# One hybrid pooling and SSD layer on one core: branch tiles loaded and split during two gate blocks, a third gate buffer, an earlier state update

## The chip, the core and the metric

The kernel runs on one core of a Trainium2 chip. The metric is the device time of one execution in microseconds (us). The kernel before was run three times: 2823.08, 2823.70 and 2825.81 us, median 2823.7. A separate execution was profiled, and its trace is what all views below come from.

The core has five engines with an instruction stream each, which wait for one another by semaphores. PE (TensorE) multiplies matrices into PSUM, DVE (VectorE) and ACT (ScalarE) work on elements, POOL (GpSimd) and SP (SyncE) mostly issue DMA transfers. [...]

## The reference

One layer of a streaming encoder is computed for 384 rows (256 of a prompt and 8 streams of 16), 2048 channels, in float32:

```
u  = RMSNorm(x);  P = u @ w_in        # pool | z | xBC | dt | gates
A  = scale * pool_w(pooling(P.pool))                      # branch A
Y  = chunked SSD scan(conv(P.xBC), dt) + d_skip * x
B  = group RMSNorm(Y * silu(z))                           # branch B
m  = sigmoid(g_A) * (A @ w_pool_proj) + sigmoid(g_B) * (B @ w_ssd_proj)
x += RMSNorm(m @ w_out)
x += RMSNorm(relu(RMSNorm(x) @ w_up)^2 @ w_down)
```

The scan's states of the running streams are updated and returned as well. The change touches the gate `sigmoid(g_B)`, the last state update of the scan, and the way branch B gets to its product with `w_ssd_proj`.

## The kernel before

Every float32 product is made of three: both operands are split into a high part (rounded to float32r by an ACT copy) and a low part (the rest, by a DVE subtraction), and PE multiplies high by high, high by low and low by high (lines 107 to 109 in `moving`, 76 to 78 in `mm3`).

**Weights.** They stream from DRAM in tiles of 128 x 1024, 512 KB each. `wfetch` (line 59) loads one over the queue of SP into one of three `w` buffers, `wsplit` (line 64) makes `wh` on ACT (line 68) and `wl` on DVE (line 69), with three buffers each. `moving` (line 99) goes through such tiles with one accumulator of 128 x 512 for each of three blocks of 128 rows (`three`, line 133): 18 matmuls a tile. After the last tile it calls `done(b)` for each block. A `hook` is a pair: after the matmuls of the tile of that number a function is called.

**Order.** The program is written with a scheduler that orders the instructions of each engine by their place in the text and by when it expects their inputs, so loads, copies and subtractions of later tiles move ahead as far as buffers allow. Matmuls of the scan stage are tied in written order (`behind`, `chain`). Memory comes from pools: a tile on the bytes of an earlier one waits for that one's users. PSUM has two banks `mm` (`mmtile`) and six banks `ss` (`sstile`), handed out in turn. `main` (line 172) holds on the right side of SBUF the input split in two (`xg`), and small tiles, among them the gate output `gbt`, two buffers.

**The stages around the change.** The scan runs over eight groups of two pairs (loop at line 776). After the last group, in the turn `g == G` (line 777):

- `dside` scales the last pair's state `hs` by its decay on DVE (line 701).
- `gate_b(0)` (line 519) multiplies `xg` with the first 512 columns of the gate weights, eight tiles. Its `done` writes the sigmoid of each of three blocks into `gbt` (ACT, line 524), and POOL stores that to DRAM, `gb_scr` (line 525).
- `state` (line 708) updates `hs`: eight small matmuls `su` into four `ss` banks (line 716), four additions on DVE (line 725), and a store on POOL (line 729). It reads `xst`, loaded by eight DMAs of SP (line 675).
- `t_yT`, `t_Y`, `t_pp` and `final` end the last pair; `gate_b(1)` follows, then `finish` (line 757), which normalises the last group and stores its four tiles of branch B in `a_scr` on POOL (line 765). The other 28 tiles are there already.
- `gate_b(2)` and `gate_b(3)`, and `main` is closed (line 859).

Then the product of branch B: 32 tiles `ar` are loaded from `a_scr` over SP (line 884) into three buffers, split into `abh` (ACT, line 887) and `abl` (DVE, line 888), which stay. Four blocks `pj_sp` with 16 weight tiles each follow (line 901), each with `ma` and `gb` read back from DRAM (lines 893 and 894), and from the second on `merge` as hook, which transposes what the block before gave.

Of the kernel before, what the change touches and what calls it, by code (L numbers as in the profile page):

```python
# [6 lines left out]
F32 = mybir.dt.float32  # L7
F32R = mybir.dt.float32r
# [6 lines left out]
P = 128  # L15
# [18 lines left out]
def build(ctx, tc, io):  # L34
# [18 lines left out]
    def sstile(name):  # L53
        return pss.tile([P, 512], F32, tag="ss", name=name)
# [44 lines left out]
    def moving(o, units, lhs, tail, done, pool=None, own=0, hook=None):  # L99
        nk = 2 * len(units)  # L100
        n = len(units)

        def mm(b, wh, wl, k, k2):
            t = slice(b * P, b * P + P)
            c = slice(k2 * 512, k2 * 512 + 512)
            mh, ml = lhs[k][0][:, t], lhs[k][1][:, t]
            te.matmul(o[b], mh, wh[:, c], start=k == 0, stop=False)  # L107
            te.matmul(o[b], mh, wl[:, c], start=False, stop=False)  # L108
            last[0] = te.matmul(o[b], ml, wh[:, c], start=False, stop=k == nk - 1)  # L109

        for kp in range(n - tail):
            wh, wl = wload(*units[kp])
            with behind(last[0] if chain[0] else None):
                for k2 in range(2):
                    for b in range(3):
                        mm(b, wh, wl, kp * 2 + k2, k2)
            if hook and kp == hook[0]:
                hook[1]()
        w = [wload(*units[kp]) for kp in range(n - tail, n - own)]
        for kp in range(n - own, n):  # L120
            f, name = wfetch(*units[kp])
            h = pool.tile([P, 1024], F32R, name=f"eh_{name}")
            l = pool.tile([P, 1024], F32R, name=f"el_{name}")
            s.activation(h, f, AF.Copy)
            v.tensor_tensor(l, f, h.bitcast(F32), ALU.subtract)
            w.append((h, l))
        for b in range(3):
            for i, (wh, wl) in enumerate(w):
                for k2 in range(2):
                    mm(b, wh, wl, (n - tail + i) * 2 + k2, k2)  # L130
            done(b)

    def three(name):
        return [sstile(f"{name}_{b}") for b in range(3)]
# [167 lines left out]
    with tc.tile_pool(name="phc", bufs=1, reuse_waits="tile") as pc, tc.tile_pool(name="phc2", bufs=2, reuse_waits="tile") as pc2:  # L302
# [174 lines left out]
        for nb in range(4):  # L477
# [3 lines left out]
            if nb == 0:  # L481
                dt_turn(srcs)

    with tc.tile_pool(name="phd", bufs=2, reuse_waits="tile") as pd, tc.tile_pool(
        name="phd1", bufs=1, reuse_waits="tile"
    ) as pd1:
# [13 lines left out]
        def conv(ui, c, tag, nb):  # L500
# [14 lines left out]
            o = pd.tile([P, T], F32, tag=tag, name=f"xs{c}", bufs=nb)  # L515
            s.activation(o, a, AF.Silu, bias=vec[:, V_CB + c : V_CB + c + 1])
            return o

        def gate_b(nb):
            o = three(f"pj_gb{nb}")  # L520

            def done(b):
                t = small.tile([P, 512], F32, tag="gbt", name=f"gbt{nb}_{b}", bufs=2)
                s.activation(t, o[b], AF.Sigmoid, scale=yx[:, b : b + 1])
                gp.dma_start(gb_scr[nb][:, b], t)

            moving(o, [(io["w_gb"][nb, kp], f"gb{nb}_{kp}") for kp in range(8)], xg, 0, done)

        def lump(fn):
            with behind(last[0]):  # L530
# [174 lines left out]
                ALU.mult,  # L705
            )

        def state(S):
            def t_su():
                hs = S.hs.rearrange("p (r h) n -> p h r n", h=2)  # L710
                for r2 in (0, 2):
                    su = [sstile(f"su{S.nm}_{r2}_{h}") for h in range(2)]
                    for r in range(2):
                        for h in range(2):
                            t = slice(h * 64, h * 64 + 64)
                            i = te.matmul(
                                su[h][:, r * 256 : r * 256 + 256],
                                S.D.bs[t, r2 + r, :],
                                S.xst[t, r2 + r, :],
                                start=True,  # L720
                                stop=True,
                            )
                    for h in range(2):
                        hr = hs[:, h, r2 : r2 + 2]
                        v.tensor_tensor(hr, hr, su[h].rearrange("p (r n) -> p r n", r=2), ALU.add)
                return i

            lump(t_su)
            gp.dma_start(io["new_ssm_s"][S.qd], S.hs)
# [46 lines left out]
        for g in range(G + 1):  # L776
            if g == G:
                dside(prev.p[1])
                gate_b(0)
                state(prev.p[1])  # L780
                py = sstile("pp_last")
                lump(lambda: t_yT(prev.p[1]))
                lump(lambda: t_Y(prev.p[1]))
                lump(lambda: t_pp(prev.p[1], py))
                final(prev.p[1])
                gate_b(1)
                finish(prev)
                break
            u0 = 17 + g * 10
            D = Pair()  # L790
            D.g = g
            D.p = [pair(D, jp) for jp in range(2)]
            D.xs, D.zs = [], []
            D.BT = conv(u0, 32 + g, "BT", 2)
            pload(D.p[0])
            if g:
                dside(prev.p[1])
            D.CT = conv(u0 + 1, 40 + g, "CT", 2)
            if g:
                state(prev.p[1])  # L800
            D.xs.append(conv(u0 + 2, g * 4, "xs", 6))
            cload(D.p[0])
            cside(D)
            D.xs.append(conv(u0 + 3, g * 4 + 1, "xs", 6))
            D.xs.append(conv(u0 + 4, g * 4 + 2, "xs", 6))
            S = D.p[0]
            lump(lambda: t_cb(D))
            mside(D)
            lump(lambda: t_trB(D))
            bside(D)  # L810
            lump(lambda: t_trx(S))
            if g:
                lump(lambda: t_yT(prev.p[1]))
                lump(lambda: t_Y(prev.p[1]))
            S.py = sstile(f"py{S.nm}")
            lump(lambda: t_yi(S))
            if g:
                lump(lambda: t_pp(prev.p[1], S.py))
            if g:
                final(prev.p[1])  # L820
            xside(S)
            D.xs.append(conv(u0 + 5, g * 4 + 3, "xs", 6))
            eside(S, 0)

            def zproj(j):
                ps = proj(in_units(u0 + 6 + j), xg, f"z{g}_{j}")
                z = pd.tile([P, T], F32, tag="zs", name=f"zs{g}_{j}", bufs=7)
                v.tensor_tensor(z, ps, rstd, ALU.mult)
                s.activation(z, z, AF.Silu)
                D.zs.append(z)  # L830

            zproj(0)
            if g:
                finish(prev)
            pload(D.p[1])
            eside(S, 1)
            zproj(1)
            dside(S)
            zproj(2)
            state(S)  # L840
            cload(D.p[1])
            zproj(3)
            S1 = D.p[1]
            lump(lambda: t_trx(S1))
            lump(lambda: t_yT(S))
            lump(lambda: t_Y(S))
            S1.py = sstile(f"py{S1.nm}")
            lump(lambda: t_yi(S1))
            lump(lambda: t_pp(S, S1.py))
            final(S)  # L850
            xside(S1)
            eside(S1, 0)
            eside(S1, 1)
            prev = D
        gate_b(2)
        gate_b(3)
        chain[0] = False
        gp.dma_start(io["new_conv"], cst_)
    main.close()

    mpool = ExitStack()
    mp = mpool.enter_context(tc.tile_pool(name="mp", bufs=1, side="right", reuse_waits="tile"))
    ms_, mtok = [], [None]

    def merge():
# [11 lines left out]
        if len(ms_) == KD:  # L877
            mp.tile([P, 120], F32, name="pad_m")

    with tc.tile_pool(name="phe", bufs=1, reuse_waits="tile") as pe1, tc.tile_pool(name="phe2", bufs=3, reuse_waits="tile") as pe2:  # L880
        ab = []
        for i in range(32):
            a = pe2.tile([P, T], F32, tag="ar", name=f"ar{i}")
            sy.dma_start(a, a_scr[i])
            h = pe1.tile([P, T], F32R, name=f"abh{i}")
            l = pe1.tile([P, T], F32R, name=f"abl{i}")
            s.activation(h, a, AF.Copy)
            v.tensor_tensor(l, a, h.bitcast(F32), ALU.subtract)
            ab.append((h, l))
        for nb in range(4):  # L890
            ma = mp.tile([P, 3, 512], F32, tag="mar", name=f"mar{nb}", bufs=1)
            gb = pe2.tile([P, 3, 512], F32, tag="gbr", name=f"gbr{nb}", bufs=1)
            sy.dma_start(ma, ma_scr[nb])
            sy.dma_start(gb, gb_scr[nb])
            o = three(f"pj_sp{nb}")
# [2 lines left out]
                v.tensor_tensor(gb[:, b], o[b], gb[:, b], ALU.mult)  # L898
                v.tensor_tensor(ma[:, b], ma[:, b], gb[:, b], ALU.add)

            moving(o, [(io["w_ssd"][nb, kp], f"sp{nb}_{kp}") for kp in range(16)], ab, 0, done, hook=(3, merge) if nb else None)
            mtok[0] = ma

    res = ctx.enter_context(tc.tile_pool(name="res", bufs=1, reuse_waits="tile"))
# [25 lines left out]
    with tc.tile_pool(name="phf", bufs=1, side="right", reuse_waits="tile") as pf, tc.tile_pool(  # L930
# [19 lines left out]
        for nb in range(4):  # L950
# [5 lines left out]
            def done(b):  # L956
# [20 lines left out]
                done,  # L977
                pk,
                5 if nb == 3 else 0,
                None if nb else (3, merge),  # L980
            )
            lastwo = last[0]
        phk.close()
# [316 lines left out]
```

## Time and profile before

| what | value |
|---|---|
| median of three runs | 2823.7 us |
| profiled execution | 2822.85 us |
| its span, first to last instruction | 2821.0 us |
| mean granted TensorE clock | 0.998 |
| PE busy | 2800.5 us |
| DVE busy | 1543.5 us |
| ACT busy | 1087.3 us |
| moved by DMA | 451.39 MB, 160 GB/s |

The gate blocks `pj_gb` run from 1204.72 to 1340.57 us of the span, with a short stretch of the scan after the first, and the first block of `pj_sp` starts at 1347.26 us.

A row of the timeline is the start, the duration (of a run of instructions, if x is over 1), the engine, the line, the operation, written tile, read tiles, shapes and count; in brackets the idle time of the engine ahead of it and whose end ended it. A row of the groups has busy time, mean duration in ns, and the idle time before. PEld is PE loading its stationary operand; SPq is the queue of SP. A matmul's duration overlaps the next one's, so the distance of two starts tells the pace.

### The profile page before, as it was taken

Reading aid. Unit: us, or ns where it says so; the run is one execution under the profiler, and the core shown is the slowest. Engines: PE = TensorE matmul, PEld = TensorE weight load, DVE = VectorE, ACT = ScalarE, POOL = GpSimd, SP = SyncE. Lnnn points to the kernel's source line nnn. Section 1 sums busy time; section 2 is a strip of 40 time slices with the busy share of each in tenths; the row PEclk is TensorE's granted clock in tenths of the full one; section 3 lists DMA queues with packets and bytes.
Section 4 is the critical chain, followed back from the end, with each engine's and each line's share of the span. In section 5 each row is a group of like instructions: output and inputs, shape, how many; then the busy total and the mean of one; then the engine's idle time right before and its main releaser. Section 6 shows DMA issues by size and latency. Waiting matters only on the chain.

```text
span 2821.0 us, 39010 instructions
## 1 busy us (share of the span) xinstructions
PE 2800.5 (99%) x15663; PEld 2546.3 (90%) x15663; DVE 1543.5 (55%) x2219; ACT 1087.3 (39%) x1586; POOL 87.5 (3%) x143
## 2 busy tenths in 40 slices
PE   9999999999999999999999999999999999999998
PEld 8998889999999999988788888989899998989897
DVE  6574336788787878844434335534444444444445
ACT  5443224454444545433422234433233333323233
POOL 0000000010000001000000000000000000000000
PEclk9999999999999999999999999999999999999999
DMA  7444445655656566544744543433434433333433
GB/s 272 131 127 143 145 139 198 204 196 183 215 202 212 192 210 200 201 160 161 236 149 149 181 154 113 142 127 127 128 127 131 129 128 127 128 127 127 128 127 126
DMA packets 140933, 451.39 MB, mean 160 GB/s; under 512 B 17808, under 2 KB 39632, under 8 KB 135760
## 3 DMA queue, kind: packets, MB, share of 16 engines
q1 hardware_dynamic: 132624, 412.97, 44.7%
q0 software_dynamic: 8128, 35.93, 3.5%
q8 instruction: 123, 2.02, 0.3%
q14 instruction: 58, 0.48, 0.1%
HBM read 407.11 MB, written 41.72 MB: 159 GB/s over the span
## 4 chain that ended last, share of the span: by engine, by line
PE 95%; issue 3%; DVE 0%; DMA 0%; POOL 0%; ACT 0%; SPq 0%; DVEq 0%; POOLq 0%; ACTq 0%
PE pj_up L77 6%; PE pj_up L78 6%; PE pj_up L76 6%; PE wd L109 6%; PE wd L108 6%; PE wd L107 6%; PE pj_x L76 5%; PE pj_x L78 5%; PE pj_x L77 5%; PE pj_z L76 3%; PE pj_z L78 3%; PE pj_z L77 3%; PE pj_sp L107 3%; PE pj_sp L108 3%; PE pj_sp L109 3%
## 5 line engine op out<-in xcount | busy, mean ns | idle before, releaser
L76 PE MATMUL pj_up<-x1h,wh_up 128*128 128x384 f32 x1024 | 342.6, 335 | 0.5 <-ACT x1h L1026 0.5
L78 PE MATMUL pj_up<-x1h,wl_up 128*128 128x384 f32 x1024 | 342.3, 334 | 0.7 <-DVE wl_up L69 0.7
L77 PE MATMUL pj_up<-x1l,wh_up 128*128 128x384 f32 x1024 | 342.3, 334 | 0.6 <-DVE x1l L1031 0.6
L69 DVE TENSOR_TENSOR wl_wd<-w_wd,wh_wd 128x1024 fp32r<-128x1024 f32 x127 | 155.7, 1226 | 261.9 <-ACT wh_wd L68 261.9
L108 PE MATMUL wd<-wl_wd,hh 128*128 128x512 f32 x762 | 296.6, 389 | 0.0
L109 PE MATMUL wd<-wh_wd,hl 128*128 128x512 f32 x762 | 296.6, 389 | 0.0
L107 PE MATMUL wd<-wh_wd,hh 128*128 128x512 f32 x762 | 296.3, 389 | 0.0
L68 ACT ACTIVATE wh_wd<-w_wd 128x1024 fp32r<-128x1024 f32 x127 | 134.9, 1062 | 350.6 <-PE wd L109 284.0
L69 DVE TENSOR_TENSOR wl_up<-w_up,wh_up 128x1024 fp32r<-128x1024 f32 x128 | 156.9, 1226 | 198.5 <-ACT wh_up L68 198.4
L68 ACT ACTIVATE wh_up<-w_up 128x1024 fp32r<-128x1024 f32 x128 | 136.0, 1063 | 323.7 <-PE pj_up L77 259.7
L76 PE MATMUL pj_x<-xgh,wh_x 128*128 128x384 f32 x768 | 258.9, 337 | 0.0
L78 PE MATMUL pj_x<-xgh,wl_x 128*128 128x384 f32 x768 | 256.6, 334 | 0.0
L77 PE MATMUL pj_x<-xgl,wh_x 128*128 128x384 f32 x768 | 256.6, 334 | 0.0
L77 PEld LDWEIGHTS pj_up<-x1l,wh_up 128*128 128x128 f32 x1024 | 192.2, 188 | 1.4 <-DVE x1l L1031 1.2
L76 PEld LDWEIGHTS pj_up<-x1h,wh_up 128*128 128x128 f32 x1024 | 192.2, 188 | 1.3 <-ACT x1h L1026 1.0
L78 PEld LDWEIGHTS pj_up<-x1h,wl_up 128*128 128x128 f32 x1024 | 192.2, 188 | 1.0 <-DVE wl_up L69 1.0
L76 PE MATMUL pj_z<-xgh,wh_z 128*128 128x384 f32 x512 | 171.9, 336 | 0.0
L78 PE MATMUL pj_z<-xgh,wl_z 128*128 128x384 f32 x512 | 171.1, 334 | 0.0
L77 PE MATMUL pj_z<-xgl,wh_z 128*128 128x384 f32 x512 | 171.0, 334 | 0.0
L108 PEld LDWEIGHTS wd<-wl_wd,hh 128*128 128x128 f32 x762 | 143.0, 188 | 29.8 <-DVE wl_wd L69 0.2
L109 PEld LDWEIGHTS wd<-wh_wd,hl 128*128 128x128 f32 x762 | 143.0, 188 | 29.7
L107 PEld LDWEIGHTS wd<-wh_wd,hh 128*128 128x128 f32 x762 | 143.0, 188 | 29.5
(318 smaller groups left out, 5729.7 us busy)
## 6 DMA issues: line engine op xcount, KB each, us to landing
w_up<-w_up SPq DMA_DIRECT2D x128, 512.0 KB, 3.4
w_wd<-w_down SPq DMA_DIRECT2D x128, 512.0 KB, 3.4
w_x<-w_in SPq DMA_DIRECT2D x96, 512.0 KB, 4.7
w_z<-w_in SPq DMA_DIRECT2D x64, 512.0 KB, 4.0
w_sp<-w_ssd SPq DMA_DIRECT2D x64, 512.0 KB, 3.4
w_ga<-w_ga SPq DMA_DIRECT2D x32, 512.0 KB, 3.5
w_pp<-w_pp SPq DMA_DIRECT2D x32, 512.0 KB, 3.4
hs<-ssm SPq DMA_DIRECT2D x16, 1024.0 KB, 6.0
```

Source lines behind the costliest of these rows:

```text
L68: s.activation(h, w, AF.Copy)
L69: v.tensor_tensor(l, w, h.bitcast(F32), ALU.subtract)
L76: te.matmul(out, wh, xh, start=first, stop=False)
L77: te.matmul(out, wh, xl, start=False, stop=False)
L78: return te.matmul(out, wl, xh, start=False, stop=last)
L107: te.matmul(o[b], mh, wh[:, c], start=k == 0, stop=False)
L108: te.matmul(o[b], mh, wl[:, c], start=False, stop=False)
L109: last[0] = te.matmul(o[b], ml, wh[:, c], start=False, stop=k == nk - 1)
```

## The change

1. `gate_b` moves ahead of the scan stage. Its output gets a pool of its own, `gbp`, with three buffers in place of two.
2. `moving` takes as hook a dictionary from tile numbers to functions.
3. The last state update is called as a hook of the first gate block, after its fifth tile (number 4). Its first two `su` tiles, and the tile `pp_last`, come from the two `mm` banks.
4. `gate_b(2)` and `gate_b(3)` move behind the end of the scan stage's pools, into the stage of branch B. After each of their 16 weight tiles a hook `aload` loads and splits two branch tiles.
5. `main` is closed, and the pool `mp` opened, after these blocks; the read-back tile `gbr` gets a pool `phe3` that opens after that.

```diff
@@ moving
-            if hook and kp == hook[0]:
-                hook[1]()
+            if hook and kp in hook:
+                hook[kp]()
@@ ahead of the scan stage
+    gbp = main.enter_context(tc.tile_pool(name="gbp", bufs=3, side="right"))
+
+    def gate_b(nb, hook=None):
+        o = three(f"pj_gb{nb}")
+
+        def done(b):
+            t = gbp.tile([P, 512], F32, tag="gbt", name=f"gbt{nb}_{b}")
+            s.activation(t, o[b], AF.Sigmoid, scale=yx[:, b : b + 1])
+            gp.dma_start(gb_scr[nb][:, b], t)
+
+        moving(o, [(io["w_gb"][nb, kp], f"gb{nb}_{kp}") for kp in range(8)], xg, 0, done, hook=hook)
@@ scan stage (the old gate_b, with bufs=2 in the pool small, goes)
-        def state(S):
+        def state(S, tiles=(sstile, sstile)):
             def t_su():
                 hs = S.hs.rearrange("p (r h) n -> p h r n", h=2)
-                for r2 in (0, 2):
-                    su = [sstile(f"su{S.nm}_{r2}_{h}") for h in range(2)]
+                for r2, tile_ in zip((0, 2), tiles):
+                    su = [tile_(f"su{S.nm}_{r2}_{h}") for h in range(2)]
...
                 dside(prev.p[1])
-                gate_b(0)
-                state(prev.p[1])
-                py = sstile("pp_last")
+                gate_b(0, {4: lambda: state(prev.p[1], (mmtile, sstile))})
+                py = mmtile("pp_last")
...
-        gate_b(2)
-        gate_b(3)
-        chain[0] = False
         gp.dma_start(io["new_conv"], cst_)
-    main.close()
-
-    mpool = ExitStack()
-    mp = mpool.enter_context(tc.tile_pool(name="mp", bufs=1, side="right", reuse_waits="tile"))
@@ stage of branch B
-        for i in range(32):
-            a = pe2.tile([P, T], F32, tag="ar", name=f"ar{i}")
-            sy.dma_start(a, a_scr[i])
-            h = pe1.tile([P, T], F32R, name=f"abh{i}")
-            l = pe1.tile([P, T], F32R, name=f"abl{i}")
-            s.activation(h, a, AF.Copy)
-            v.tensor_tensor(l, a, h.bitcast(F32), ALU.subtract)
-            ab.append((h, l))
+
+        def aload():
+            for i in (len(ab), len(ab) + 1):
+                a = pe2.tile([P, T], F32, tag="ar", name=f"ar{i}")
+                sy.dma_start(a, a_scr[i])
+                h = pe1.tile([P, T], F32R, name=f"abh{i}")
+                l = pe1.tile([P, T], F32R, name=f"abl{i}")
+                s.activation(h, a, AF.Copy)
+                v.tensor_tensor(l, a, h.bitcast(F32), ALU.subtract)
+                ab.append((h, l))
+
+        for nb in (2, 3):
+            gate_b(nb, {kp: aload for kp in range(8)})
+        chain[0] = False
+        main.close()
+        mp = mpool.enter_context(tc.tile_pool(name="mp", bufs=1, side="right", reuse_waits="tile"))
+        pe3 = phe.enter_context(tc.tile_pool(name="phe3", bufs=1, reuse_waits="tile"))
         for nb in range(4):
             ma = mp.tile([P, 3, 512], F32, tag="mar", name=f"mar{nb}", bufs=1)
-            gb = pe2.tile([P, 3, 512], F32, tag="gbr", name=f"gbr{nb}", bufs=1)
+            gb = pe3.tile([P, 3, 512], F32, tag="gbr", name=f"gbr{nb}")
```

More of the change, by code (lines that the diff above doesn't have):

```diff
@@ L517, in conv @@
             return o
[L519 to L527, printed above, removed]
         def lump(fn):
@@ L878, in merge @@
             mp.tile([P, 120], F32, name="pad_m")
-    with tc.tile_pool(name="phe", bufs=1, reuse_waits="tile") as pe1, tc.tile_pool(name="phe2", bufs=3, reuse_waits="tile") as pe2:
+    mpool = ExitStack()
+    with ExitStack() as phe:
+        pe1 = phe.enter_context(tc.tile_pool(name="phe", bufs=1, reuse_waits="tile"))
+        pe2 = phe.enter_context(tc.tile_pool(name="phe2", bufs=3, reuse_waits="tile"))
         ab = []
-        for i in range(32):
-            a = pe2.tile([P, T], F32, tag="ar", name=f"ar{i}")
-            sy.dma_start(a, a_scr[i])
-            h = pe1.tile([P, T], F32R, name=f"abh{i}")
-            l = pe1.tile([P, T], F32R, name=f"abl{i}")
-            s.activation(h, a, AF.Copy)
-            v.tensor_tensor(l, a, h.bitcast(F32), ALU.subtract)
-            ab.append((h, l))
+        def aload():
[13 more added lines that the diff above has]
+        pe3 = phe.enter_context(tc.tile_pool(name="phe3", bufs=1, reuse_waits="tile"))
         for nb in range(4):
             ma = mp.tile([P, 3, 512], F32, tag="mar", name=f"mar{nb}", bufs=1)
-            gb = pe2.tile([P, 3, 512], F32, tag="gbr", name=f"gbr{nb}", bufs=1)
+            gb = pe3.tile([P, 3, 512], F32, tag="gbr", name=f"gbr{nb}")
             sy.dma_start(ma, ma_scr[nb])
@@ L899, in done @@
                 v.tensor_tensor(ma[:, b], ma[:, b], gb[:, b], ALU.add)
-            moving(o, [(io["w_ssd"][nb, kp], f"sp{nb}_{kp}") for kp in range(16)], ab, 0, done, hook=(3, merge) if nb else None)
+            moving(o, [(io["w_ssd"][nb, kp], f"sp{nb}_{kp}") for kp in range(16)], ab, 0, done, hook={3: merge} if nb else None)
             mtok[0] = ma
@@ L979, in build @@
                 5 if nb == 3 else 0,
-                None if nb else (3, merge),
+                None if nb else {3: merge},
             )
```

## The prediction

> **What bounds the kernel now.** I read the page first, then the list of waits, then the timeline at the two places of the change.
>
> ```profile
> PE 2800.5 (99%) x15663; PEld 2546.3 (90%) x15663; DVE 1543.5 (55%) x2219; ACT 1087.3 (39%) x1586; POOL 87.5 (3%) x143
> ...
> PE 95%; issue 3%; DVE 0%; DMA 0%; POOL 0%; ACT 0%; SPq 0%; DVEq 0%; POOLq 0%; ACTq 0%
> ```
>
> PE is busy for 2800.5 of 2821.0 us and makes up 95% of the chain that ended last. The change removes no matmul, so all it can win is PE idle time (20.5 us in the whole span) and matmuls that run slowly after an idle stretch. The list of waits says where one large piece lies (total us, times, longest):
>
> ```profile
> ACT abh L887 <- DMA ar<-a_scr: 22.2, 13, 2.9
> ...
> PE pj_sp L107 <- ACT abh L887: 6.7, 1, 6.7
> ```
>
> The second row is the largest PE wait that the list names: 6.7 us, once, before the first branch product. The timeline around it:
>
> ```profile
> 1339.24 1.37 ACT L524 ACTIVATE gbt<-pj_gb,yx 128x512 f32<-128x512 f32 x2 [1.66 <-PE pj_gb L109]
> ...
> 1339.30 1.33 SPq L884 DMA_DIRECT2D ar<-a_scr  x3
> ...
> 1340.18 0.39 PE L109 MATMUL pj_gb<-wh_gb,xgl 128*128 128x512 f32 x1
> 1340.23 1.22 POOL L525 DMA_DIRECT2D gb_scr<-gbt  x2 [27.01 <-ACT gbt L524]
> ...
> 1346.11 0.69 ACT L524 ACTIVATE gbt<-pj_gb,yx 128x512 f32<-128x512 f32 x1 [4.45 <-DMA gb_scr<-gbt]
> 1346.69 1.34 ACT L887 ACTIVATE abh<-ar 128x384 fp32r<-128x384 f32 x3
> ...
> 1347.26 0.79 PE L107 MATMUL pj_sp<-wh_sp,abh 128*128 128x512 f32 x1 [6.69 <-ACT abh L887]
> ...
> 1351.17 0.40 PE L107 MATMUL pj_sp<-wh_sp,abh 128*128 128x512 f32 x1
> ```
>
> The last gate block ends on PE at 1340.57 (1340.18 + 0.39). Its third sigmoid needs one of two gbt buffers, and those are still being written to DRAM; ACT stands in order behind that until 1346.11, and the first branch copy (abh) stands behind the sigmoid. The branch loads were themselves only issued at 1339.30. PE starts at 1347.26, and nine steps bring it to 1351.17, 0.43 us each.
>
> **The change part by part.** *The wait before the branch product.* With branch tiles split ahead and a buffer for each sigmoid, the tenth pj_sp matmul (1351.17) would start ten ordinary steps after the last pj_gb start. One weight tile is 18 matmuls and takes 4.09 us (weight copies at 1332.44 and 1336.53, quoted below, each let go by PE), so a step is 0.227: 1340.18 + 2.27 = 1342.45. That is 8.72 us gained: 6.85 of idle (1347.26 against 1340.41) and 1.87 of slow steps. The bounds are nothing, if another wait ends as late, and 8.72.
>
> The windows show the slow steps as a lower granted clock (columns: PE, PEld, DVE, ACT, POOL busy and count; clock; DMA share; GB/s):
>
> ```profile
> 1276.00:1309.00 33.00, 33.00 (x147) 27.32 (x146) 16.84 (x22) 10.54 (x12) 3.78 (x7) 1.00 0.53 177
> 1309.00:1340.30 31.30, 31.30 (x140) 25.81 (x138) 9.81 (x8) 9.09 (x11) 0.61 (x2) 1.00 0.44 144
> 1340.30:1347.30 7.00, 0.31 (x3) 0.04 (x1) 1.28 (x2) 2.56 (x5) 1.22 (x3) 0.78 0.91 336
> 1347.30:1364.00 16.70, 16.70 (x66) 13.70 (x67) 8.30 (x13) 7.67 (x13) 0.33 (x1) 0.89 0.79 266
> 1364.00:1420.00 56.00, 56.00 (x249) 46.39 (x248) 31.50 (x43) 24.66 (x35) 0.00 (x0) 1.00 0.65 199
> ```
>
> The clock is 1.00 in the gate blocks and 0.78 and 0.89 around the wait. [...]
>
> *The last state update, moved after the fifth of eight weight tiles of gate block 0.* Where it stands now, and the same eight matmuls inside a stream of projections:
>
> ```profile
> 1190.56 0.33 PE L77 MATMUL pj_z<-xgl,wh_z 128*128 128x384 f32 x1
> 1190.73 0.34 PE L78 MATMUL pj_z<-xgh,wl_z 128*128 128x384 f32 x1
> 1191.00 0.75 PE L716 MATMUL su<-xst,bst 64*128 64x256 f32 x8
> ...
> 1191.95 0.34 PE L77 MATMUL pj_z<-xgl,wh_z 128*128 128x384 f32 x1
> ```
>
> ```profile
> 1236.33 1.37 ACT L524 ACTIVATE gbt<-pj_gb,yx 128x512 f32<-128x512 f32 x2 [0.36 <-PE pj_gb L109]
> ...
> 1237.27 0.39 PE L109 MATMUL pj_gb<-wh_gb,xgl 128*128 128x512 f32 x1
> ...
> 1237.58 0.74 PE L716 MATMUL su<-xst,bst 64*128 64x256 f32 x8
> ...
> 1238.12 2.48 DVE L725 TENSOR_TENSOR hs<-hs,su 128x512 f32<-128x512 f32 x4 [2.19 <-PE su L716]
> ...
> 1238.87 0.44 PE L587 MATMUL Y<-cst,yis 128*128 128x128 f32 x2 [0.54 <-DVE hs L725]
> ```
>
> From the last gate matmul to Y is 1.60 us now; 0.54 of it PE waits for DVE, since Y takes a PSUM bank that the state update holds. Inside a stream the update costs 1191.95 - 1190.73 = 1.22 less two ordinary steps of 0.17 (1190.56 to 1190.73) = 0.88. Gate to Y then takes one step plus the 0.08 of the change of kind (1237.58 - 1237.27 - 0.23), 0.31. So 1.60 - 0.88 - 0.31 = 0.41 us gained; the ends are nothing (the update waits inside the block) and 0.54. In the new place Y's second bank is that of the block's first sigmoid, done at 1237.02 (1236.33 + half of 1.37), before Y can start. The update's inputs:
>
> ```profile
> 1209.60 4.14 SPq L675 DMA_DIRECT2D xst<-x_scr  x8
> ...
> 1210.59 2.29 DVE L701 TENSOR_TENSOR hs<-hs,decb 128x2048 f32<-128x2048 f32 x1
> ```
>
> Issued by 1213.74 and scaled by 1212.88; the new place is three tiles before 1237.3, about 1225, so 11 us are left for the landing. The four DVE additions (2.48 us) and the state store on POOL move 12 us forward with it; DVE, busy 55% of the span, has room for them.
>
> *Branch tiles in gate blocks 2 and 3.* Work is moved, none added: 32 loads on SP, 32 copies on ACT, 32 subtractions on DVE, two of each per weight tile, against what the weights cost already:
>
> ```profile
> L69 DVE TENSOR_TENSOR wl_gb<-w_gb,wh_gb 128x1024 fp32r<-128x1024 f32 x32 | 39.1, 1224 | 66.4 <-ACT wh_gb L68 66.4
> ...
> L888 DVE TENSOR_TENSOR abl<-ar,abh 128x384 fp32r<-128x384 f32 x32 | 16.7, 556 | 19.4 <-ACT abh L887 19.4
> ...
> L887 ACT ACTIVATE abh<-ar 128x384 fp32r<-128x384 f32 x32 | 15.9, 523 | 22.2 <-DMA ar<-a_scr 22.2
> ```
>
> Per 4.09 us: ACT 1.06 (the weight copy) + 2 x 0.52 = 2.1, DVE 1.22 + 2 x 0.56 = 2.34. In block 2, with the normalisation, DVE has 16.84 + 16 x 0.56 = 25.7 of 33 us. Sixteen loads of 197 KB in 33 us add 95 GB/s to 177 and 144; the chip gave 266 in the first stretch of pj_sp and 336 in the wait. So throughput suffices, and the question is order. A branch copy that waits for its load holds the next weight copy behind it on ACT, with it the weight subtraction on DVE, the release of the weight buffer to SP, and PE at the end. The margin can be read, and so can what the same mix made of it in pj_sp:
>
> ```profile
> 1332.44 1.06 ACT L68 ACTIVATE wh_sp<-w_sp 128x1024 fp32r<-128x1024 f32 x1 [3.02 <-PE pj_gb L109]
> 1336.53 1.06 ACT L68 ACTIVATE wh_sp<-w_sp 128x1024 fp32r<-128x1024 f32 x1 [3.02 <-PE pj_gb L109]
> ...
> 1369.74 1.06 ACT L68 ACTIVATE wh_sp<-w_sp 128x1024 fp32r<-128x1024 f32 x1 [0.17 <-PE pj_sp L109]
> ...
> 1397.70 1.04 ACT L68 ACTIVATE wh_sp<-w_sp 128x1024 fp32r<-128x1024 f32 x1
> ```
>
> The split that starts at 1332.44 ends at about 1334.8 and is used at 1340.41: 5.6 us of margin. From 1369.74 to 1397.70 six further splits ran with three branch tiles each, 4.66 us apiece against PE's 4.09: the split fell 3.4 us behind, and PE was busy 56.00 of 56.00 us. So the cost in gate blocks is nothing if two tiles go with each split (three buffers in 4.66 us allow 2.6 per 4.09). If all 32 run three to a split it is 10.7 x 0.57 = 6.1, 0.5 beyond the margin; with three sigmoids in between (half of 1.37 each, 2.1) and, as an estimate, two DVE instructions of 0.56 from the normalisation in the way (1.1), it is 3.7. I take nothing, by the row of 56.00, and keep 3.7 for the range.
>
> **Sum.** 8.72 + 0.41 = 9.1 us. The profiled execution took 2822.85 us (span 2821.0), 0.85 below the median of 2823.7; from the median, 2814.6. Faster here means by over 0.2%, 5.6 us, below 2818.1; within that bound a measurement of this kernel can't tell it from no change.
>
> **The rivals.** *Slower: a loop closes through SP and ACT.* If the program's order puts the two branch loads behind the weight load that waits for a buffer, and the branch copies ahead of the weight copy that frees it, each weight tile runs: three issues (about 0.4 each, from 1.33 for three), landing, two copies (1.05), weight copy (1.06), subtraction (1.22). Issue and landing:
>
> ```profile
> L884 SPq DMA_DIRECT2D ar<-a_scr x32: 319/320/423, 1339.3 to 1393.9; - x32
> ...
> DMA to landing us min/median/max: 2.7/3.6/5.4
> ```
>
> With 3.6 for the landing (2.7 to 5.4) that is 8.1 us against 4.09. Over all 16 tiles PE loses 16 x 4.0 - 5.6 = 58 us and the kernel takes 2823.7 + 58 - 9 = 2873; it turns slower once about four tiles run so ((9.1 + 5.6) / 4.0), beyond the bound from five. Against it: in pj_sp the branch loads stood one step ahead, and ACT waited 2.9 us for one at the longest. For it: loads now alternate strictly with weights, and ACT is in order. [...]
>
> *The wait shrinks but stays.* Branch tiles lie on bytes of the tiles before them. Where another stage changes, its first loads come late (SP rows and PE rows of one timeline):
>
> ```profile
> 1613.17 1.37 SPq L929 DMA_DIRECT2D x<-x_tok  x3
> ...
> 1614.10 0.39 PE L109 MATMUL pj_sp<-wh_sp,abl 128*128 128x512 f32 x1
> ```
>
> The next stage's x1 comes only as the last pj_sp matmul is near, though DMA had room. If the branch loads still begin at 1339.30, only the sigmoid's wait goes: the first tile lands by 1342.9 to 1344.7 and PE starts after one copy, 1343.4 to 1345.2, 2.1 to 3.9 us earlier than now. With 0.4 that is 2.5 to 4.3, so 2819.4 to 2821.2, unless the shorter gap also saves the 1.87. A softer form, loads only from the middle of block 2, near 1293, needs 32 x 1.55 (4.66 / 3) = 50 us, to 1343: no loss, as product k needs only tiles 2k and 2k + 1.
>
> *A new wait eats part.* The gate rows read back for pj_sp (gbr) now lie, by the order in which the pools open and close, on bytes of the gate output buffers, so their load may hold SP until the last gate store has landed, with the fourth weight tile of pj_sp behind it.
>
> ```profile
> w_sp<-w_ssd SPq DMA_DIRECT2D x64, 512.0 KB, 3.4
> ```
>
> With T the end of the last gate block, the third sigmoid ends at T + 1.4, the store takes at most 5.9 (1340.23 to 1346.11) and SP is free at about T + 7.3. The fourth tile is used at T + 12.3 and needs 3.4 to land and 2.4 to split: 0.8 late. With the 3.7 of stalls above that takes 4.5 and leaves 4.6: 2819.1.
>
> **How the numbers follow.** The forecast has 0.73; it lies from 2813.0 (0.13 more from the state update, 0.85 for the profiled run under the median, 0.6 for the spread of the runs below it) to 2818.3 (3.7 of stalls alone), all but 0.01 of it below the bound. The wait that stays has 0.07 and the new wait with the stalls 0.06, both within 0.2%; the loop 0.14, of which 0.12 is beyond the bound. So faster 0.72, same 0.01 + 0.07 + 0.06 + 0.02 = 0.16, slower 0.12. The range runs from 2813.0 to 2821.5: it takes in the unknown costs and both small rivals and leaves out the loop.
>
> **What would show it.** Right: no PE wait before pj_sp, clock 1.00 there, ar loads between 1270 and 1345, no DVE row before Y, PE idle 20.5 less 7. Wrong: rows of PE pj_gb or pj_sp waiting for wl or wh (the loop), or for abh (the wait stays); weight copies on ACT more than 5.6 us behind their matmuls.

## The result and the profile after

The kernel after takes 2815.86 us (median of 8 runs, 2814.26 to 2816.16), the kernel before 2824.14 in 8 runs beside it (2822.28 to 2826.31): 8.3 us less, a ratio of 0.9969 with a 95% interval from 0.9958 to 0.9980. The profiled execution took 2816.05 us, with a span of 2814.3. The page of the kernel after, first the busy times, then the shares of the chain that ended last:

```profile
PE 2800.4 (100%) x15663; PEld 2546.4 (90%) x15663; DVE 1544.6 (55%) x2219; ACT 1085.1 (39%) x1586; POOL 88.2 (3%) x143
...
PE 98%; DMA 1%; DVE 0%; ACT 0%; SPq 0%; issue 0%; DVEq 0%; ACTq 0%
```

PE has the same 15663 matmuls; idle time fell to 2814.3 - 2800.4 = 13.9 us where it was 20.5. That the busy time looks unchanged is a coincidence of this trace: the slow steps at the seam are gone, but a later stretch ran slowly (last section). In e3, e4 and e9 below, which have neither, PE is busy 2798.3 to 2798.6 us. The waits of the kernel after (total us, times, longest) no longer have a row of pj_sp; the longest PE wait is at the warm-up, and only ACT's wait for the branch loads is left:

```profile
ACT abh L887 <- DMA ar<-a_scr: 20.7, 16, 2.1
...
PE warm_o L187 <- POOL warm L183: 1.3, 1, 1.3
```

The seam between the last gate block and the first branch product, on PE of the kernel after:

```profile
1340.44 0.39 PE L109 MATMUL pj_gb<-wh_gb,xgl 128*128 128x512 f32 x1
1340.66 0.39 PE L107 MATMUL pj_sp<-wh_sp,abh 128*128 128x512 f32 x1
1340.89 0.39 PE L108 MATMUL pj_sp<-wl_sp,abh 128*128 128x512 f32 x1
```

From the last gate matmul to the first branch matmul it was 7.08 us; now it is 0.22, one ordinary step. The windows (columns as in the prediction) show what the branch tiles do in the gate blocks:

```profile
1275.00:1309.00 34.00, 34.00 (x152) 28.19 (x151) 23.78 (x36) 15.39 (x24) 3.63 (x7) 1.00 0.72 237
1309.00:1340.00 31.00, 31.00 (x139) 25.66 (x138) 18.41 (x27) 18.28 (x30) 1.62 (x3) 1.00 0.78 253
1340.00:1360.00 20.00, 20.00 (x90) 16.57 (x89) 7.88 (x7) 7.22 (x9) 1.62 (x3) 1.00 0.80 276
```

PE is full and the clock is 1.00 throughout; in the second stretch DVE rises from 9.81 to 18.41 us, ACT from 9.09 to 18.28, and DMA moves 253 GB/s in place of 144. When the branch tiles are really split is read from ACT and DVE:

```profile
1291.90 1.06 ACT L68 ACTIVATE wh_gb<-w_gb 128x1024 fp32r<-128x1024 f32 x1 [1.78 <-PE pj_gb L109]
1295.11 1.51 ACT L887 ACTIVATE abh<-ar 128x384 fp32r<-128x384 f32 x3 [2.15 <-DMA ar<-a_scr]
...
1336.95 1.46 ACT L887 ACTIVATE abh<-ar 128x384 fp32r<-128x384 f32 x3 [1.77 <-DMA ar<-a_scr]
1338.31 1.99 ACT L68 ACTIVATE wh_sp<-w_sp 128x1024 fp32r<-128x1024 f32 x2
...
1339.39 2.36 DVE L69 TENSOR_TENSOR wl_sp<-w_sp,wh_sp 128x1024 fp32r<-128x1024 f32 x2 [0.39 <-ACT wh_sp L68]
```

The code asks for two tiles with each of 16 weight tiles, but ACT takes them mostly three at a time with ten weight copies. From 1291.90 to 1338.31 these ten took 46.41 us, PE's ten tiles take 40.9, so the splits fell back 5.5 us. The first `wl_sp` is ready at about 1340.57 (1339.39 + half of 2.36) and is used at 1340.89: 0.3 us of cover are left.

To compare the whole stretch that the change touches, I take the distance from the last group of `cb` matmuls (scan) to the first transposes of `merge`, and then from the fourth such transposes to the last `z`. First the kernel before, then the kernel after:

```profile
1151.35 1.04 PE L556 MATMUL cb<-xs,xs 128*128 128x256 f32 x6
...
1430.74 1.48 PE L871 MATMUL tr_m<-cst,mar 128*128 128x128 f32 x12
...
1630.65 1.47 PE L871 MATMUL tr_m<-cst,mar 128*128 128x128 f32 x12
...
2816.66 0.74 DVE L1165 SCALAR_TENSOR_TENSOR z<-z,n_n,x 128x512 f32<-128x512 f32 x1
```

```profile
1152.16 1.04 PE L558 MATMUL cb<-xs,xs 128*128 128x256 f32 x6
...
1422.27 1.47 PE L866 MATMUL tr_m<-cst,mar 128*128 128x128 f32 x12
...
1622.21 1.47 PE L866 MATMUL tr_m<-cst,mar 128*128 128x128 f32 x12
...
2809.92 0.74 DVE L1172 SCALAR_TENSOR_TENSOR z<-z,n_n,x 128x512 f32<-128x512 f32 x1
```

The stretch is 279.39 before and 270.11 after: 9.28 us gained. Ahead of it the profiled execution of the kernel after was 0.81 later, and its last part took 1187.71 in place of 1186.01, so the two spans differ by 6.7 only. Neither is put down to the change: the `cb` rows start between 1151.28 and 1153.20 in the traces below, whichever kernel they come from, and the last part has two lengths with both kernels (last section). This stretch is the ruler for the experiments below; each has one trace, so a difference in it is that of two executions.

### The profile page after: what moved, and what is told of

It reads as the page before. It is cut to its first block, busy times and chain, and to the rows that moved or that the text cites. A ratio compares the mean times of both kernels' runs of the same rounds, so it can differ in the third digit from the quotient of the medians.

```text
span 2814.3 us, 39013 instructions
## 1 busy us (share of the span) xinstructions
PE 2800.4 (100%) x15663; PEld 2546.4 (90%) x15663; DVE 1544.6 (55%) x2219; ACT 1085.1 (39%) x1586; POOL 88.2 (3%) x143
## 4 chain that ended last, share of the span: by engine, by line
PE 98%; DMA 1%; DVE 0%; ACT 0%; SPq 0%; issue 0%; DVEq 0%; ACTq 0%
PE pj_up L77 6%; PE pj_up L78 6%; PE pj_up L76 6%; PE wd L108 6%; PE wd L109 6%; PE wd L107 6%; PE pj_x L76 5%; PE pj_x L78 5%; PE pj_x L77 5%; PE pj_z L76 3%; PE pj_z L78 3%; PE pj_z L77 3%; PE pj_sp L107 3%; PE pj_sp L108 3%; PE pj_sp L109 3%; PE pj_gb L107 2%
## 5 line engine op out<-in xcount | busy, mean ns | idle before, releaser
L109 PE MATMUL wd<-wh_wd,hl 128*128 128x512 f32 x762 | 296.6, 389 | 0.0
L109 PEld LDWEIGHTS wd<-wh_wd,hl 128*128 128x128 f32 x762 | 143.0, 188 | 29.7
```

## The experiments

**e1: the state update alone.** The kernel before, with only part 3 of the change.

```diff
-                gate_b(0)
-                state(prev.p[1])
-                py = sstile("pp_last")
+                gate_b(0, (4, lambda: state(prev.p[1], (mmtile, sstile))))
+                py = mmtile("pp_last")
```

> The kernel before with the earlier state update alone (hook after tile 4 of gate block 0, its first two su tiles and pp_last in the mm banks). My account: last matmul of gate block 0 to the first Y matmul shrinks from 1.60 us to about 0.3, the block itself grows by about 0.8, so 0.4 to 0.5 us are gained; the wait of 6.7 us before pj_sp and the slow steps behind it stay. Rival (the state update was holding more, for instance through POOL's or DVE's order): the wait before pj_sp gets shorter as well.

Measured: 2822.4 us in one run, beside 2823.46 for the kernel before; one run settles nothing, but the stretch of its trace is 0.52 us shorter. Nearer by, from the last group of `cb` to the first Y matmul behind gate block 0 it is 87.03 us, in the kernel before 87.52. The wait before pj_sp stays:

```profile
PE pj_sp L107 <- ACT abh L886: 6.6, 1, 6.6
```

So the early update is worth half a microsecond, and the wait is not its affair.

**e2: the third gate buffer alone.** The kernel before, with `gbt` in a pool of three.

```diff
+    gbp = main.enter_context(tc.tile_pool(name="gbp", bufs=3, side="right"))
...
-                t = small.tile([P, 512], F32, tag="gbt", name=f"gbt{nb}_{b}", bufs=2)
+                t = gbp.tile([P, 512], F32, tag="gbt", name=f"gbt{nb}_{b}")
```

> The kernel before with three gate output buffers in a pool of their own, and nothing else of the change. My account (two causes in a row, the sigmoid's wait and then the late branch loads): the sigmoid's wait goes, but the branch loads still start near 1339.3 and need 3.6 us (2.7 to 5.4) to land, so pj_sp starts near 1343.4 to 1345.2 instead of 1347.26: 2.1 to 3.9 us gained, up to 1.9 more if the shorter gap leaves the clock alone; time ratio 0.998 to 0.9992. Rival (the third buffer is the whole gain, the branch loads ride along): pj_sp starts right behind the gate block, 8 to 9 us gained, ratio 0.997.

Measured: 2827.08 us (2826.25 to 2830.07) against 2823.46, ratio 1.0016 (1.0007 to 1.0025), the stretch 2.04 us longer. Both theories missed: it is slower. The wait list, and then ACT and SP of e2:

```profile
PE pj_sp L107 <- ACT abh L888: 9.0, 1, 9.0
```

```profile
1339.46 2.05 ACT L525 ACTIVATE gbt<-pj_gb,yx 128x512 f32<-128x512 f32 x3 [1.66 <-PE pj_gb L109]
...
1339.47 0.42 SPq L894 DMA_DIRECT2D mar<-ma_scr  x1
1343.74 0.33 SPq L61 DMA_DIRECT2D w_sp<-w_ssd  x1
1344.16 1.66 SPq L885 DMA_DIRECT2D ar<-a_scr  x3
```

The sigmoid's wait is gone (three in one go, 2.05 us), but the scheduler has put SP in another order: mar and the sixth weight tile, which must wait for a weight buffer until 1343.74, stand ahead of the first branch tiles. These are issued at 1344.16 instead of 1339.30. The buffer freed ACT, and an engine nobody had meant to touch lost more.

**e8: the weight load held back.** e2, with the sixth `w_sp` load tied behind the third branch load on SP.

```diff
+        with behind(ar2[0] if name == "sp0_5" else None):
             sy.dma_start(w, src)
...
-            sy.dma_start(a, a_scr[i])
+            d = sy.dma_start(a, a_scr[i])
+            if i == 2:
+                ar2[0] = d
```

> The kernel before with the third gbt buffer alone, as in e2, but with the sixth w_sp load held behind the load of the third branch tile in SP's order; all else as in e2. Theory: e2 lost because the first three branch loads stood on SP behind that weight load, which waits for a buffer. With them ahead of it they are issued at about 1339.5 to 1340, land 1.5 to 2.9 us later, and ACT, free from about 1342.4, copies the first then; PE starts pj_sp at 1343 to 1345 instead of 1349.7 in e2 and 1347.3 before. The PE wait before pj_sp falls from 9.0 to 2.5 to 4.5 us, and the time is 2 to 5 us under the kernel before (ratio 0.9982 to 0.9993). Rival: the order on SP is not what cost the time (the third write of gbt beside the loads is, or the clock); then the wait stays at 6.5 us or more and the time is at or above the kernel before (ratio 1.000 or more).

Measured: 2825.86 us (2823.96 to 2828.17), ratio 1.0007 (0.9998 to 1.0016), the stretch 0.51 longer than before. The theory's 2.5 to 4.5 us of wait missed as well; it is 6.1. SP and ACT of e8:

```profile
1341.10 0.42 SPq L899 DMA_DIRECT2D mar<-ma_scr  x1
1341.62 1.59 SPq L888 DMA_DIRECT2D ar<-a_scr  x3
...
1347.98 0.52 ACT L893 ACTIVATE abh<-ar 128x384 fp32r<-128x384 f32 x1 [3.90 <-DMA ar<-a_scr]
```

(This execution is 1.85 us later than that of the kernel before by its `cb` rows.) The branch loads are now issued while the gate block still runs, but the first tile is copied only 6.4 us after its issue, with the 768 KB of mar ahead of it (e10 puts mar behind; there the first copy starts at 1343.71, 3.74 us after the issue at 1339.97). Some of the shorter wait is also lost again later: four steps between 1391.41 and 1396.77, where PE has caught up with the weight splits, are 0.8 us too long together.

**e10: nearly the order of the kernel before, with three buffers.** e8, with mar tied behind the third branch load too.

```diff
+            with behind(None if nb else ar2[0]):
                 sy.dma_start(ma, ma_scr[nb])
```

> The kernel before with the third gbt buffer, with both the load of mar (768 KB) and the sixth w_sp load held behind the first three branch loads in SP's order, which is the order that the kernel before has; e8 held only the weight load back. Theory: in e8 the first branch tile took 6.4 us from its issue (1341.62) to its copy (1347.98), because mar, issued 0.5 us ahead of it, and the writes of gbt share the DMA engines with it. With mar behind, the first tile lands 3.5 to 5 us after its issue, the PE wait before pj_sp falls from 6.1 to 2.5 to 4.5 us, and the time is 2 to 4 us under the kernel before (ratio 0.9985 to 0.9993). Rival: the three writes of gbt (768 KB at about the same moment) alone hold the branch tiles back as long as that; the wait stays at 5 us or more and the time within 0.1% of the kernel before. Either way it stays 4 us or more behind the kernel after, which starts pj_sp with no wait.

Measured: 2823.01 us (2820.59 to 2824.63) against 2824.07, ratio 0.9994 (0.9985 to 1.0003), the stretch 0.71 us shorter. The wait fell as the theory said, the time hardly. PE of e10, the rows with idle time and the ends of the slow steps, then its weight copies on ACT:

```profile
1340.85 0.39 PE L112 MATMUL pj_gb<-wh_gb,xgl 128*128 128x512 f32 x1
1344.29 0.50 PE L110 MATMUL pj_sp<-wh_sp,abh 128*128 128x512 f32 x1 [3.05 <-ACT abh L893]
...
1348.62 0.40 PE L112 MATMUL pj_sp<-wh_sp,abl 128*128 128x512 f32 x1
...
1375.54 0.50 PE L111 MATMUL pj_sp<-wl_sp,abh 128*128 128x512 f32 x1 [0.29 <-DVE wl_sp L72]
...
1384.64 0.50 PE L110 MATMUL pj_sp<-wh_sp,abh 128*128 128x512 f32 x1 [0.56 <-ACT wh_sp L71]
1385.90 0.50 PE L111 MATMUL pj_sp<-wl_sp,abh 128*128 128x512 f32 x1 [0.76 <-DVE wl_sp L72]
```

```profile
1352.79 1.04 ACT L71 ACTIVATE wh_sp<-w_sp 128x1024 fp32r<-128x1024 f32 x1
...
1395.70 1.99 ACT L71 ACTIVATE wh_sp<-w_sp 128x1024 fp32r<-128x1024 f32 x2
```

PE starts 3.44 us after the last gate matmul instead of 7.08. But nine weight splits with the branch tiles between them take 42.91 us, 4.77 each against PE's 4.09, and as PE started earlier it catches up with them: from 1374.86 to 1386.24 seven steps are longer than ordinary, by 2.7 us together. What was won at the seam was paid back 30 us later. The long wait of the kernel before had been covering this lag. One difference in SP's order remains: the second three branch loads stand behind mar in e10 (1341.36, then 1344.86), in the kernel before behind gbr (1340.79, then 1347.83), a load of the same size; what it is worth was not tried.

**e3: the kernel after with two gate buffers.**

```diff
-    gbp = main.enter_context(tc.tile_pool(name="gbp", bufs=3, side="right"))
+    gbp = main.enter_context(tc.tile_pool(name="gbp", bufs=2, side="right"))
```

> The changed kernel with two gate output buffers in place of three. My account: branch tiles are split ahead, so the first matmul of pj_sp no longer stands behind the third sigmoid; that sigmoid still waits about 4 to 5 us on ACT and delays only the third weight copy of pj_sp, which has most of a 5.6 us margin: 0 to 1.5 us lost against the changed kernel, ratio to the kernel before 0.997 to 0.9975. Rival (both parts are needed): the wait before or early in pj_sp comes back with 4 us or more, ratio above 0.9985.

Measured: 2815.35 us (2814.29 to 2816.62), ratio 0.9971 (0.9959 to 0.9982), as the kernel after; the stretch is 0.66 us longer than its. One PE wait is new, for a weight split in the last gate block:

```profile
PE pj_gb L108 <- DVE wl_gb L69: 0.3, 1, 0.3
```

The third buffer isn't needed once the first branch tiles are split before the last sigmoid; at most this fraction of a microsecond hangs on it.

**e4: the kernel after with the state update where it was.**

```diff
-                gate_b(0, {4: lambda: state(prev.p[1], (mmtile, sstile))})
-                py = mmtile("pp_last")
+                gate_b(0)
+                state(prev.p[1])
+                py = sstile("pp_last")
```

> The changed kernel with the last state update back behind gate block 0 (four ss banks, pp_last in an ss bank). My account: 0.4 to 0.5 us slower than the changed kernel, seen as a PE wait of about 0.5 us for the DVE addition of hs before Y; everything later is the same, pj_sp follows the gate block without a wait. Rival (the earlier update is what lets the branch loads start, since it frees their bytes sooner): the first branch loads move from 1221 to behind 1238 and the wait before pj_sp comes back in part.

Measured: 2815.01 us (2814.64 to 2815.56), ratio 0.9968 (0.9957 to 0.9980), which timing alone can't tell from the kernel after. From `cb` to Y it is 87.52 us as before, against 87.03 in the kernel after, and PE's wait for DVE ahead of Y is back:

```profile
PE Y L589 <- DVE hs L727: 0.5, 1, 0.5
```

The rival is right in one half: the first three branch loads move from 1220.93 to 1236.83. It costs nothing here, since their copies start at 1288.97, in the kernel after at 1288.79, and no wait before pj_sp comes back.

**e5, e6, e7: one, two and four branch buffers.** The kernel after; only the number changes (1 shown).

```diff
-                a = pe2.tile([P, T], F32, tag="ar", name=f"ar{i}")
+                a = pe2.tile([P, T], F32, tag="ar", name=f"ar{i}", bufs=1)
```

> The changed kernel with one buffer for the loaded branch tiles in place of three. In the program one branch copy then stands between two weight copies on ACT, over some 28 weight tiles. My account (weight copies are paced by the turnaround of a branch buffer, issue, landing, copy, subtraction, about 4.7 us against PE's 4.09, so each such weight tile costs 0.5 to 0.6 us of a margin of 5.6): 28 x 0.55 - 5.6 = about 10 us of PE waits in pj_gb and pj_sp, so about as slow as the kernel before, ratio 0.999 to 1.002. Rival (a single tile has the DMA queues to itself and lands faster, so the pace of PE is kept): no PE wait, ratio 0.997.

> The changed kernel with two buffers for the loaded branch tiles. Two branch copies then stand between two weight copies, over some 16 weight tiles. My account (same pace of 4.7 us against 4.09): 16 x 0.55 plus 1 to 2 us for the sigmoids is 10 to 11 us, less the margin of 5.6: 4 to 5 us of PE waits, ratio 0.9985. Rival (margin is not used up, pace of PE is kept): no PE wait, ratio 0.997.

> The changed kernel with four buffers for the loaded branch tiles. Three to four branch copies stand between two weight copies, over some 10 weight tiles. My account: 10 x 0.55 plus the sigmoids is inside the margin of 5.6 or at its edge, so no PE wait or under 1 us, the same time as the changed kernel, with the last weight copy before pj_sp less late than in the changed kernel. Rival (what counts is ACT's and DVE's work between two weight tiles, 4 x 0.52 + 1.06 and 4 x 0.56 + 1.22): weight copies fall behind faster than with three, and PE waits 1 us or more.

| branch buffers | us (range) | ratio to before (interval) | stretch against before |
|---|---|---|---|
| 1 (e5) | 2827.94 (2825.91 to 2830.68) | 1.0012 (1.0003 to 1.0021) | +4.46 |
| 2 (e6) | 2819.17 (2816.32 to 2820.12) | 0.9980 (0.9970 to 0.9989) | -5.83 |
| 3 (after) | 2815.86 (2814.26 to 2816.16) | 0.9969 (0.9958 to 0.9980) | -9.28 |
| 4 (e7) | 2816.30 (2813.69 to 2817.97) | 0.9970 (0.9959 to 0.9982) | -8.33 |

With one buffer PE isn't late in the gate blocks, where I had expected it; it runs out of branch tiles in pj_sp. Its waits there, one window and ACT:

```profile
PE pj_sp L107 <- ACT abh L887: 5.7, 3, 2.7
PE pj_sp L107 <- ACT wh_sp L68: 2.1, 2, 1.1
```

```profile
1400.00:1425.00 25.00, 20.75 (x72) 15.84 (x73) 5.90 (x8) 5.46 (x8) 0.00 (x0) 0.80 0.34 106
```

```profile
1406.43 1.06 ACT L68 ACTIVATE wh_sp<-w_sp 128x1024 fp32r<-128x1024 f32 x1 [4.30 <-PE pj_sp L109]
1407.39 0.51 ACT L887 ACTIVATE abh<-ar 128x384 fp32r<-128x384 f32 x1
...
1417.62 1.06 ACT L68 ACTIVATE wh_sp<-w_sp 128x1024 fp32r<-128x1024 f32 x1 [3.93 <-PE pj_sp L109]
```

One tile goes with each weight split, about 4.1 us a turn (24 splits from 1291.36 to 1389.29), so the weight splits keep up, but the product needs two branch tiles per 4.09 us. At the end the streams lock in one another: the weight copy waits for PE, the branch copy stands behind it on ACT, PE waits for the branch copy; 11.2 us from one weight copy to the next (1406.43 to 1417.62). With two buffers the ten splits from 1291.03 to 1336.14 take 45.11 us, a lag of 4.2, so the gate blocks pass without a wait. But ten branch tiles are still to come, and the five weight splits among them take 24.71 us (to 1360.85), 4.94 each. PE then waits for weight splits, not for branch tiles:

```profile
PE pj_sp L108 <- DVE wl_sp L69: 2.2, 3, 0.8
```

The expected direction held for e6 (the rival, no wait, fell) and e7 (within 1 us). Three is about the best of the four: with fewer buffers too few branch tiles are split before pj_sp. A fourth brings nothing: PE waits 0.2 us for a `wl_gb` in the gate blocks, and the stretch is 0.95 us longer than with three.

**e9: the hooks put later.** The kernel after, with no branch tiles asked for in gate block 2 and four instead of two per weight tile in block 3.

```diff
-            for i in (len(ab), len(ab) + 1):
+            for i in range(len(ab), len(ab) + 4):
...
-        for nb in (2, 3):
-            gate_b(nb, {kp: aload for kp in range(8)})
+        gate_b(2)
+        gate_b(3, {kp: aload for kp in range(8)})
```

> The kernel after, with the branch tiles not handed out two per weight tile in the last two gate blocks but four per weight tile in the very last one. Theory: where the hooks stand doesn't set when the tiles are loaded; the planner moves each up to where a buffer is free, so the loads keep the order of the kernel after (three tiles per weight tile, from near 1289 to 1338), and the time is that of the kernel after within 1 us (ratio 0.9962 to 0.9980 to the kernel before). Rival: the tiles follow the hooks, so 32 tiles crowd into 8 weight tiles; at 4.65 us per three tiles they take 50 us from about 1307 to 1357, and PE waits in pj_sp or for the last weight tiles by 3 to 9 us (ratio 0.998 to 1.001).

Measured: 2814.75 us (2813.49 to 2815.14), ratio 0.9964 (0.9951 to 0.9977), the stretch 0.73 us longer than in the kernel after, and the time the same within the interval. The 0.73 is nearly all at the seam, where PE waits 0.4 us for the first `wl_sp`, a small part of what the rival expected. SP of e9 issues the second three branch tiles at the same moment as the kernel after (1290.64 there), although the text first asks for any in gate block 3, which starts near 1308 (eight tiles of 4.09 ahead of its end):

```profile
1290.46 1.34 SPq L884 DMA_DIRECT2D ar<-a_scr  x3
```

As the theory said, the scheduler moves the tiles up, whatever their place in the text. What holds the first of them is memory, by SP's list of waits: in the kernel before line 884 waits once for PE's `pj_gb` (L109, 0.2 us), in the kernel after once for PE's `su` (L718, 5.6 us), which reads `xst`. So the reading, which no run tests alone, is that the change gave the branch tiles bytes that come free before the gate blocks end.

## Why the prediction was right

The forecast was 2814.6 us and 9.1 us of gain; 2815.86 and 8.3 were measured, and the ratio's interval (5.6 to 11.9 us of 2824.14) holds the 9.1.

1. *The wait and the slow steps, 8.72.* Right. The seam shrank by 7.08 - 0.22 = 6.86 us, and the clock is 1.00 behind it. With the 0.49 of the next point taken off, the stretch gives 9.28 - 0.49 = 8.79.
2. *The state update, 0.41.* Right in kind, a little small: 87.52 - 87.03 = 0.49, the same alone (e1) and within the change (e4). Now from the last matmul of gate block 0 to Y is one step, without the 0.08 that I had added:

```profile
1238.96 0.39 PE L109 MATMUL pj_gb<-wh_gb,xgl 128*128 128x512 f32 x1
1239.19 0.38 PE L589 MATMUL Y<-cst,yis 128*128 128x128 f32 x2
```

3. *No stall in the gate blocks.* The result was right, the reason was not. I expected two tiles with each split, so no lag, by the row of 56.00 busy of 56.00. The tiles went three at a time and the splits fell back 5.5 us. What I had kept only for the range (three to a split, 6.1 us against 5.6 of margin) is what happened, and it passed by 0.3 us. That was partly luck: e3, e7 and e9 shift the copies a little, and each has PE waits of 0.2 to 0.4 us for a `wl` and a stretch that is 0.66 to 0.95 us longer. The two additions on top (2.1 for sigmoids, 1.1 for the normalisation) did not show in the sum.
4. *The loop through SP and ACT.* Not in the kernel after. A loop of this kind is real, though: it closes in e5, at 11.2 us a turn in place of the 8.1 that I had worked out, for two turns near the end.
5. *The wait shrinks but stays.* Its softer form is how the loads fell out: copies from 1288.79 to 1338.4, 50 us, without loss, as worked out. Its harder form, only the sigmoid's wait gone, was built in e10: PE started at 1344.29, which is 1343.62 on the clock of the kernel before (its last gate matmul starts 0.67 earlier, at 1340.18 instead of 1340.85), inside the 1343.4 to 1345.2 given. But the price of 2.1 to 3.9 us was wrong: 0.7 remained. The step that failed there is the same as in point 3. I had treated an earlier start of PE as free, while it uses up the margin by which the splits are ahead. That a shorter gap would also save the 1.87 of slow steps no run shows: after 3.05 us of idling in e10 they cost 1.83.
6. *gbr holds SP.* It does, but costs nothing here. SP of the kernel after:

```profile
1342.16 0.48 SPq L900 DMA_DIRECT2D mar<-ma_scr  x1
...
1351.12 0.33 SPq L901 DMA_DIRECT2D gbr<-gb_scr  x1
```

SP stood until 1351.12, 10.3 us after the end of the last gate matmul (7.3 was estimated), but no matmul of pj_sp waits.

So the cause, as the runs show it: with the branch tiles loaded inside pj_sp, 32 tiles at about 1.6 us each are a chain of 50 us. Three go with a weight split, so PE needs only 43.6 us for the weight tiles among them (10.7 of 4.09 us), and it waits at the start (before, e2), further on (e10) or at both places (e8). The change runs this chain 58 us earlier (copies from 1288.79 instead of 1346.69), beside gate matmuls that don't need it. The third buffer contributes nothing that the times show (e3) and alone costs time (e2) or brings almost nothing (e10); the state update brings half a microsecond (e1, e4). No run leaves out both at once, but each of e3 and e4 keeps nearly the whole gain, and what the two lose is under 0.7 us each.

What stays open: why the scheduler reorders SP when one more gate buffer is there. That it does is shown; the reason was not looked into. The moved pools (part 5 of the change) were not tried alone either.

## What to carry to other kernels

A wait at a seam may hide a slower stream behind it: before you price its removal, compare the pace of the loads and splits that follow with PE's, and how far ahead they are. Move the whole stream to a place where PE doesn't need it, and not only its first tile. After a small change such as one more buffer, read the order on each engine's queue again: the gain on one engine can be lost on another (in e2 SP issued the first branch loads at 1344.16 instead of 1339.30).

## What the runs showed of the hardware

**Slow steps followed an idle gap of 3.05 us already.** In e10 PE idled 3.05 us (3.44 from start to start, 3.21 more than a step), and eleven steps from 1344.29 to 1348.62 took 4.33 us, where 2.5 are ordinary. The windows of e10:

```profile
1341.30:1344.20 2.90, 0.00 (x0) 0.00 (x0) 1.22 (x1) 2.10 (x3) 1.22 (x3) 1.00 0.84 276
1344.20:1348.60 4.40, 4.31 (x11) 3.22 (x12) 1.68 (x3) 1.08 (x3) 0.00 (x0) 0.62 0.99 377
```

The first three of these steps take 0.34, 0.25 and 0.34 us, the eight from 1345.22 to 1348.62 0.42 or 0.43 each. In e5 no wait before a pj_sp matmul is longer than 2.7 us (its waits above), and yet the clock from 1400.00 to 1425.00 is 0.80. In the window ahead of that it is 1.00, though PE idled there too, 3.67 of 20.00 us:

```profile
1380.00:1400.00 20.00, 16.33 (x68) 12.08 (x66) 7.61 (x9) 6.73 (x9) 0.00 (x0) 1.00 0.53 162
```

The slow steps cost 1.83 us after 3.05 us of idling (e10), 1.73 after 6.14 (e8), 1.87 after 6.69 (before) and 1.56 after 8.98 (e2): in these four runs the price doesn't follow the length of the gap.

**A late stretch ran at either of two lengths.** The last part, from the fourth transposes to the last `z`, took 1187.6 to 1187.7 us in four of the twelve profiled executions (the kernel after, e5, e7, e10) and 1186.0 to 1186.2 in the other eight. The kernel after, then e3, after the same stretch of small transposes in which PE is busy 3.1 of 4.6 us:

```profile
1738.20:1742.80 4.60, 3.08 (x24) 2.34 (x22) 3.27 (x10) 2.94 (x9) 0.00 (x0) 1.00 0.02 4
1742.80:1747.80 5.00, 5.00 (x21) 4.97 (x22) 3.72 (x10) 2.69 (x8) 0.00 (x0) 0.66 0.00 0
```

```profile
1742.80:1747.80 5.00, 5.00 (x32) 4.96 (x32) 3.72 (x10) 3.57 (x12) 0.00 (x0) 1.00 0.00 0
```

The clock over these 5 us is 0.66 in the one and 1.00 in the other, and 1.00 in the kernel before (1751.20 to 1756.20 of its span). In e7, another long execution, the matmuls of this place (`pj_up`, 1743.68 to 1744.64) follow each other at 0.31 to 0.33 us, in the kernel before (from 1751.69) at 0.17 to 0.18. What decides was not tried; both happen with kernels that are the same in this part. For the reader of two profiles it means that 1.7 us of a difference in span can have nothing to do with the change, which is why the experiments were compared by the stretch.
